# Layer 0's split activations moved to two areas with their own offsets in each stage, in a float32r decoder trunk

## The chip, the cores and the metric

The kernel runs on one core of a Trainium2 chip. The metric is the device time of one execution in microseconds. Before the change it is 2354.8 us, the median of three runs (2354.66 to 2355.55).

## What is computed

The reference is a decoder trunk of two layers over 272 tokens (16 meta tokens and 256 inputs) of width 2048, in float32. Layer 0 is a self-decoder with forgetting attention, layer 1 a cross-decoder with stick-breaking attention over a shared K/V; each is followed by a squared-ReLU MLP.

```python
D_MODEL = 2048; SEQ = 256; DEPTH = 2; N_HEADS = 16; D_FF = 4 * D_MODEL; N_META = 16

def squared_relu_mlp(h, w_up, w_down):
    u = h @ w_up
    return jnp.square(jax.nn.relu(u)) @ w_down

def reference(...):
    h = jnp.concatenate([meta, x], axis=1)
    for layer in range(DEPTH):
        a = rms_norm(h, norm_attn[layer])
        if layer < N_A_LAYERS:
            proj = a @ fox_w_in[i]
            q, k, v, f_logit = jnp.split(proj, [D_MODEL, 2 * D_MODEL, 3 * D_MODEL], axis=-1)
            ...
            o = forgetting_attention(split_heads(q), split_heads(k), split_heads(v), cum_logf)
            h = h + o.reshape(b, length, D_MODEL) @ fox_w_o[i]
        else:
            if layer == N_A_LAYERS:
                c = rms_norm(h, kv_norm)
                k_s, v_s = jnp.split(c @ w_kv, 2, axis=-1)
            ...
            q = split_heads(a @ sb_w_q[i])
            o = stick_breaking_attention(q, shared_k, shared_v)
            h = h + o.reshape(b, length, D_MODEL) @ sb_w_o[i]
        h = h + squared_relu_mlp(rms_norm(h, norm_mlp[layer]), w_up[layer], w_down[layer])
    return rms_norm(h, final_norm)[:, N_META:]
```

Nearly all of the arithmetic is in the products with the weight matrices.

## The kernel before

Activations lie feature-major in SBUF: the 128 partitions hold 128 features, a "chunk" c is one of 16 blocks of 128 features, and the tokens (272, or 256 where the meta tokens are no longer needed) run along the free dimension. `hT` is the residual stream.

To get float32 accuracy out of float32r products, each operand is split into a high part rounded to float32r and a low part with the rest, and a product W x is computed as three: whi·xhi + whi·xlo + wlo·xhi. An activation that feeds such products is a `Split` (L117): a tile of the pool `xs` (two buffers, tag "x") of 16 rows, one for each chunk, XROW = 576 floats (2304 bytes) apart. In each row hi starts at float XHI = 16 and lo follows directly after the n tokens of hi; `both` is the two together. `split_chunk` (L127) fills one chunk from hT: hi on ScalarE (L130), lo on VectorE (L131). `put_split` (L334) fills rows from attention outputs, and the evacuation of the MLP's up projection (L466) fills them from the squared ReLU.

The Splits by stage, in order: `a0` (input of layer 0's Q, K, V), `o0` (attention output, input of its projection), `m0` (input of the MLP's up projection), `u0_0` to `u0_3` (four quarters of the hidden layer, inputs of the down projection), then `a1` (256 tokens, queries of layer 1), `kv` (272 tokens, shared K and V), and layer 1's `o1`, `m1`, `u1_0` to `u1_3`, all of 256 tokens. a0, m0 and a1 lie in the first buffer of `xs`, o0, u0_0 to u0_3 and kv in the second.

`gemm_group` (L169) computes one group: 512 output features (four accumulators m of 128 features, in four PSUM banks) from all 2048 input features. It loads the weights in four blocks kb of 1 MB (`raw`, queue of SyncE), splits each half of a block into `whi` on ScalarE (L205) and `wlo` on VectorE (L206), and then runs over chunk kc and accumulator m. The variable `u` numbers the groups: 1 to 12 for Q, K, V of layer 0 (q, k, v for each of four groups of heads), 13 to 16 for its projection, 17 to 48 for its MLP (four quarters of four up and four down groups), 49 to 52 for layer 1's queries, 53 to 60 for K and V, the rest for layer 1. With 272 tokens (n = 272, a0 to u0_3 and kv) each (chunk, accumulator) takes three matmuls of 272 columns: L228 (whi, hi), L229 (whi, lo), L230 (wlo, hi); I call them a triple. There are 56 such groups of 64 triples, 3584 triples or 10752 matmuls. With 256 tokens (`pairs`) it takes two: L225 (whi, `both`, 512 columns) and L226 (wlo, hi, 256 columns). The framework's scheduler decides the final order on each engine within the data dependences, so L228 and L229 of several accumulators are sometimes grouped.

The forget gates (L281) multiply the same rows of a0 with weights of 16 columns, `wf_hi` and `wf_lo`, in three matmuls for each chunk (L286 to L288).

Addresses within a partition (bytes), as the framework allots them: the first buffer of `xs` starts at 91392, the second at 128256, both multiples of 256. So hi of every row starts 64 bytes past a multiple of 256; lo, 1088 bytes later where n is 272, starts at 128 past a multiple of 256. The weights `whi` and `wlo` start at multiples of 256 (66816, 79104 and on), and each 128x128 block of them is 512 bytes a partition; the gates' weights lie 64 bytes apart from chunk to chunk.

Of the kernel before, what the change touches and what calls it, by code (L numbers as in the profile page):

```python
# [9 lines left out]
F32 = mybir.dt.float32  # L10
F32R = mybir.dt.float32r
# [4 lines left out]
P = 128  # L16
D = 2048
NC = D // P
# [6 lines left out]
N_FF = 4  # L25
XROW = 576
XHI = 16

G_A0, G_M0, G_KV, G_A1, G_M1, G_FIN = range(6)

# [2 lines left out]
def yoco_kernel(ctx: ExitStack, tc: tile.TileContext, hT_in, gains, b_f, w_f, w_qkv0, w_o0, w_up, w_dn,  # L33
                w_kv, w_q1, w_o1, outT):
    nc = tc.nc
# [6 lines left out]
    xs = ctx.enter_context(tc.tile_pool(name="xs", bufs=2))  # L42
# [74 lines left out]
    class Split:  # L117


        def __init__(self, label, t0):  # L120
            n = T - t0
            self.t0 = t0
            rows = xs.tile([P, NC, XROW], F32R, tag="x", name=f"x_{label}")
            self.hi, self.lo = rows[:, :, XHI:XHI + n], rows[:, :, XHI + n:XHI + 2 * n]
            self.both = rows[:, :, XHI:XHI + 2 * n]

    def split_chunk(sp, gi, c):  # L127

# [40 lines left out]
    def gemm_group(wblk, sp, t0, evac, before={}, after={}, load_x=None, pairs=False, apart=()):  # L169

        uid[0] += 1
        u = uid[0]
        accs = [pacc.tile([P, 512], F32, tag="acc", name=f"acc_{u}_{m}") for m in range(4)]
        n = T - t0
        for kb in range(4):
            raw = wraw.tile([P, 4, 512], F32, tag="raw", name=f"raw_{u}_{kb}")  # L180
            src_w = wblk[kb].rearrange("p (k c) -> p k c", k=4)
            if kb in before:
                before[kb]()
            piece = 4 if load_x is None else (1, 2, 2, 4)[kb]
            for k0 in range(0, 4, piece):
                if load_x is not None:
                    load_x(range(4 * kb + k0, 4 * kb + k0 + piece))
                if load_x is not None and kb == k0 == 0:

                    for c0 in (0, 256):  # L190
                        nc.scalar.dma_start(raw[:, 0, c0:c0 + 256], src_w[:, 0, c0:c0 + 256])
                else:
                    nc.sync.dma_start(raw[:, k0:k0 + piece], src_w[:, k0:k0 + piece])
            piece = min(piece, 2)
            parts = []
            for hf in range(2):
                whi = wspl.tile([P, 2, 512], F32R, tag="whi", name=f"whi_{u}_{kb}_{hf}")
                wlo = wspl.tile([P, 2, 512], F32R, tag="wlo", name=f"wlo_{u}_{kb}_{hf}")
                boxes = [(o, piece, 0, 512) for o in range(0, 2, piece)]
                if load_x is not None and kb == hf == 0:  # L200
                    boxes[:1] = [(0, 1, 0, 256), (0, 1, 256, 512)]
                for o, no, c0, c1 in boxes:
                    src = raw[:, 2 * hf + o:2 * hf + o + no, c0:c1]
                    hp, lp = whi[:, o:o + no, c0:c1], wlo[:, o:o + no, c0:c1]
                    on_act = nc.scalar.activation(hp, src, AF.Copy)  # L205
                    on_dve = nc.vector.tensor_tensor(out=lp, in0=src, in1=hp.bitcast(F32), op=ALU.subtract)  # L206
                parts.append((whi, wlo))
            if kb in after:
                with tc.issue_after(on_act.ins), tc.issue_after(on_dve.ins):
                    after[kb]()  # L210
            order = [(kc, m) for hf in range(2) for m in range(4) for kc in range(2 * hf, 2 * hf + 2)]
            if load_x is not None and kb == 0:
                order = [(kc, m) for kc in range(4) for m in range(4)]
            if kb == 3:
                order = [(kc, m) for m in range(4) for kc in range(4)]
            for kc, m in order:
                whi, wlo = parts[kc // 2]
                k = 4 * kb + kc
                wh = whi[:, kc % 2, m * P:(m + 1) * P]
                wl = wlo[:, kc % 2, m * P:(m + 1) * P]  # L220
                first = kb == 0 and kc == 0
                last = kb == 3 and kc == 3
                hi, lo = sp.hi[:, k], sp.lo[:, k]
                if pairs and m not in apart:
                    nc.tensor.matmul(accs[m], wh, sp.both[:, k], start=first, stop=False)  # L225
                    nc.tensor.matmul(accs[m][:, :n], wl, hi, start=False, stop=last)  # L226
                else:
                    nc.tensor.matmul(accs[m][:, :n], wh, hi, start=first, stop=False)  # L228
                    nc.tensor.matmul(accs[m][:, :n], wh, lo, start=False, stop=False)  # L229
                    nc.tensor.matmul(accs[m][:, :n], wl, hi, start=False, stop=last)  # L230
                if last:
                    evac(m, [accs[m][:, :n]] + ([accs[m][:, n:]] if pairs and m not in apart else []))
# [18 lines left out]
    def load_x(chunks):  # L251
        c0, n = chunks[0], len(chunks)
        nc.sync.dma_start(hT[:, c0:c0 + n, :], hT_in[:, c0:c0 + n, :])
        if c0 == 0:
            nc.sync.dma_start(g_sb, gains)
        for c in chunks:
            split_chunk(xa, G_A0, c)
# [82 lines left out]
    for g in range(4):  # L340
# [11 lines left out]
        if g == 0:  # L352
            gemm_group(w_qkv0[0], xa, 0, evac_q, after={kb: (lambda kb=kb: first_norm(kb)) for kb in range(4)}, load_x=load_x)
            forget_gates(box["rstd"])
        else:
            gemm_group(w_qkv0[3 * g], xa, 0, evac_q)
# [4 lines left out]
        def decays(j):  # L361

            for i, (o, n) in enumerate(((0, 144), (144, T))):
                nc.vector.scalar_tensor_tensor(out=s[:, j, o:o + n], in0=fk[:, j, :n],
                                               scalar=fq_sb[:, i, 4 * g + j:4 * g + j + 1],
                                               in1=maskA[:, o:o + n], op0=ALU.subtract, op1=ALU.add)

        gemm_group(w_qkv0[3 * g + 1], xa, 0, lambda m, acc: evac_kv(m, acc, kT),
                   after={j: (lambda j=j: decays(j)) for j in range(4)})

# [255 lines left out]
    a, y, t, rs = (fin[:, i, :] for i in range(4))  # L626
# [9 lines left out]
    for i in range(2):  # L636
        pr = patt.tile([P, 512], F32, tag="patt", name=f"pr_fin_{i}")
        for b in range(2):
            nc.tensor.matmul(pr[:, b * P:(b + 1) * P], rs[:, b:b + 1].to_broadcast([P, P]), ident,
                             start=True, stop=True)  # L640
        prs.append(pr[:, :S])
    ob = xs.tile([P, NC, XROW], F32, tag="x", name="ob")
    pr_sb = tmp.tile([P, T], F32, tag="relu", name="pr_sb")[:, :S]
    nc.scalar.copy(pr_sb, prs[1])
    for c, n in [(12, 1), (13, 1), (14, 1), (15, 1), (0, 2), (2, 2), (4, 2), (6, 2)]:
# [62 lines left out]
```

## Time and profile before

| | |
|---|---|
| median of three runs | 2354.8 us |
| profiled execution | 2355.27 us |
| its span, first to last instruction | 2353.6 us |
| granted TensorE clock, mean | 0.998 |
| TensorE busy | 2339.7 us, 99% |
| VectorE busy | 1343.7 us, 57% |
| ScalarE busy | 1056.2 us, 45% |
| DMA | 411.9 MB, mean 175 GB/s |

By stage, from the trace's first and last start on each Split:

| stage | Split | from, us | to, us | matmuls |
|---|---|---|---|---|
| Q, K, V of layer 0, with attention | a0 | 5.3 | 336.3 | 2304 |
| its projection | o0 | 336.4 | 436.2 | 768 |
| MLP up, four quarters | m0 | 436.3 | 1105.7 | 3072 |
| MLP down, four quarters in between | u0_0 to u0_3 | 532.4 | 1201.3 | 4 x 768 |
| queries of layer 1 | a1 | 1201.4 | 1293.1 | 512 |
| K, V of layer 1, with attention | kv | 1293.2 | 1521.6 | 1536 |
| layer 1's projection and MLP | o1, m1, u1_0 to u1_3 | 1521.7 | 2339.8 | 512 + 2048 + 4 x 512 + 16 |

A matmul's reported length includes a drain that overlaps the next one; the distance from one start to the next is what it costs the engine.

### The profile page before, as it was taken

How to read it: one execution, taken by the hardware profiler on the slowest of the kernel's cores; microseconds unless marked ns; L12 is line 12 of the kernel's file. 1: busy time of each engine (PE TensorE's matmuls, PEld its weight loads, DVE VectorE, ACT ScalarE, POOL GpSimd, SP SyncE). 2: the span in 40 equal slices, each digit the busy share in tenths (PEclk: the TensorE clock that was granted, in tenths of full speed). 3: DMA queues.
4: the chain of work that ended last, by engine and by line, in shares of the span. 5: the costliest groups of instructions: out<-in, count | busy, mean ns of one | idle time of the engine just before them, and what ended most of it. 6: DMA issues, size and time to landing. Idle time of an engine off the chain costs nothing.

```text
span 2353.6 us, 39103 instructions
## 1 busy us (share of the span) xinstructions
PE 2339.7 (99%) x16496; PEld 2207.5 (94%) x16496; DVE 1343.7 (57%) x1920; ACT 1056.2 (45%) x1471; POOL 33.4 (1%) x58
## 2 busy tenths in 40 slices
PE   9999999999999999999999999999999999999998
PEld 9999999999999999999998999988888888888887
DVE  7565555655454455455566555566555655655665
ACT  5434344544343344344445444445544543543543
POOL 1000000000000000000000000000000000000000
PEclk9999999999999999999999999999999999999999
DMA  6444444544555454545545444445545555455453
GB/s 231 157 157 171 171 162 162 179 176 168 178 177 179 171 188 162 186 172 179 180 162 196 162 145 143 146 175 179 193 178 186 196 179 197 174 187 196 178 197 125
DMA packets 61040, 411.92 MB, mean 175 GB/s; under 512 B 7089, under 2 KB 10049, under 8 KB 12097
## 3 DMA queue, kind: packets, MB, share of 16 engines
q1 hardware_dynamic: 58976, 406.27, 48.6%
q10 hardware_dynamic: 1888, 3.16, 0.4%
q8 instruction: 129, 2.11, 0.4%
q14 instruction: 47, 0.38, 0.0%
HBM read 407.29 MB, written 2.11 MB: 174 GB/s over the span
## 4 chain that ended last, share of the span: by engine, by line
PE 99%; DVE 0%; ACT 0%; DMA 0%; issue 0%; DVEq 0%; SPq 0%; ACTq 0%
PE acc L225 25%; PE acc L228 19%; PE acc L229 19%; PE acc L230 19%; PE acc L226 13%; PE ps L376 0%; PE pza L555 0%; PE pv L315 0%; PE po L438 0%; PE po L594 0%; PE pzb L556 0%; PE po L595 0%; PE po L439 0%; DMA g_sb<-gains 0%; ACT whi L205 0%; PE po L596 0%
## 5 line engine op out<-in xcount | busy, mean ns | idle before, releaser
L206 DVE TENSOR_TENSOR wlo<-raw,whi 128x1024 fp32r<-128x1024 f32 (+1 forms) x771 | 932.9, 1220 | 751.8 <-ACT whi L205 748.6
L205 ACT ACTIVATE whi<-raw 128x1024 fp32r<-128x1024 f32 (+1 forms) x771 | 803.2, 1054 | 1064.5 <-PE acc L229 669.8
L225 PE MATMUL acc<-x_m,whi 128*128 128x512 f32 x1024 | 343.2, 394 | 0.5 <-DVE relu L243 0.5
L225 PE MATMUL acc<-x_u,whi 128*128 128x512 f32 x1008 | 338.0, 394 | 0.0
L228 PE MATMUL acc<-x_u,whi 128*128 128x272 f32 (+1 forms) x1040 | 297.7, 289 | 0.0
L229 PE MATMUL acc<-x_u,whi 128*128 128x272 f32 (+1 forms) x1040 | 294.8, 286 | 0.0
L228 PE MATMUL acc<-x_m,whi 128*128 128x272 f32 x1024 | 293.4, 289 | 0.0
L229 PE MATMUL acc<-x_m,whi 128*128 128x272 f32 x1024 | 290.4, 286 | 0.0
L230 PE MATMUL acc<-x_u,wlo 128*128 128x272 f32 (+1 forms) x1040 | 285.2, 284 | 0.0
L230 PE MATMUL acc<-x_m,wlo 128*128 128x272 f32 x1024 | 280.7, 284 | 0.0
L226 PE MATMUL acc<-x_m,wlo 128*128 128x256 f32 x1024 | 252.7, 282 | 0.0
L226 PE MATMUL acc<-x_u,wlo 128*128 128x256 f32 x1008 | 247.6, 281 | 0.0
L228 PE MATMUL acc<-x_a,whi 128*128 128x272 f32 x768 | 222.6, 294 | 0.8 <-ACT x_a L130 0.8
L229 PE MATMUL acc<-x_a,whi 128*128 128x272 f32 x768 | 220.2, 291 | 0.0
L225 PEld LDWEIGHTS acc<-x_m,whi 128*128 128x128 f32 x1024 | 185.0, 188 | 30.3 <-DVE relu L243 0.9
L230 PE MATMUL acc<-x_a,wlo 128*128 128x272 f32 x768 | 211.2, 288 | 0.0
L226 PEld LDWEIGHTS acc<-x_m,wlo 128*128 128x128 f32 x1024 | 192.3, 188 | 19.6 <-DVE wlo L206 4.7
L225 PEld LDWEIGHTS acc<-x_u,whi 128*128 128x128 f32 x1008 | 182.4, 188 | 29.8
L226 PEld LDWEIGHTS acc<-x_u,wlo 128*128 128x128 f32 x1008 | 189.3, 188 | 15.8 <-DVE wlo L206 1.5
L228 PEld LDWEIGHTS acc<-x_u,whi 128*128 128x128 f32 x1040 | 195.5, 188 | 0.2
L229 PEld LDWEIGHTS acc<-x_u,whi 128*128 128x128 f32 x1040 | 195.1, 188 | 0.1
L228 PEld LDWEIGHTS acc<-x_m,whi 128*128 128x128 f32 x1024 | 192.5, 188 | 0.0
(249 smaller groups left out, 3601.3 us busy)
## 6 DMA issues: line engine op xcount, KB each, us to landing
raw<-w_up SPq DMA_DIRECT2D x128, 1024.0 KB, 4.8
raw<-w_dn SPq DMA_DIRECT2D x128, 1024.0 KB, 4.8
raw<-w_qkv SPq DMA_DIRECT2D x45, 1024.0 KB, 4.8
raw<-w_o SPq DMA_DIRECT2D x32, 1024.0 KB, 4.8
raw<-w_kv SPq DMA_DIRECT2D x32, 1024.0 KB, 4.8
raw<-w_q SPq DMA_DIRECT2D x16, 1024.0 KB, 4.9
fk<-f_dram ACTq DMA_DIRECT2D x4, 544.0 KB, 5.7
raw<-w_qkv SPq DMA_DIRECT2D x4, 512.0 KB, 8.2
```

The costliest lines, as they stand in the source:

```text
L205: on_act = nc.scalar.activation(hp, src, AF.Copy)
L206: on_dve = nc.vector.tensor_tensor(out=lp, in0=src, in1=hp.bitcast(F32), op=ALU.subtract)
L225: nc.tensor.matmul(accs[m], wh, sp.both[:, k], start=first, stop=False)
L226: nc.tensor.matmul(accs[m][:, :n], wl, hi, start=False, stop=last)
L228: nc.tensor.matmul(accs[m][:, :n], wh, hi, start=first, stop=False)
L229: nc.tensor.matmul(accs[m][:, :n], wh, lo, start=False, stop=False)
L230: nc.tensor.matmul(accs[m][:, :n], wl, hi, start=False, stop=last)
```

## The change

Splits named in `FIRST_ROWS` (all with 272 tokens) get another layout: hi in one area of the tile and lo in a second area, in both with rows 288 floats (1152 bytes) apart. hi's area starts a floats into the tile, lo's area XLO + b = 4672 + b floats into it; each Split has its own pair (a, b), with a of 0 or 16 and b of 0, 16, 32 or 48, so that each of the eight pairs occurs once. The other Splits keep their rows, cut out of the now larger tile (9344 floats and not 9216). In `gemm_group`, groups of 272 tokens with an even number u multiply whi with lo first and then with hi; groups with an odd number keep the order hi, lo. The final output tile `ob`, of the same pool, is cut to the old shape.

```diff
+FIRST_ROWS = {"a0": (16, 32), "o0": (0, 16), "m0": (16, 48), "u0_0": (0, 32), "u0_1": (16, 0), "u0_2": (0, 48),
+              "u0_3": (16, 16), "kv": (0, 0)}
+XLO = 4672
+XSIZE = XLO + 64 + NC * 288
...
-            rows = xs.tile([P, NC, XROW], F32R, tag="x", name=f"x_{label}")
-            self.hi, self.lo = rows[:, :, XHI:XHI + n], rows[:, :, XHI + n:XHI + 2 * n]
-            self.both = rows[:, :, XHI:XHI + 2 * n]
+            rows = xs.tile([P, XSIZE], F32R, tag="x", name=f"x_{label}")
+            if label in FIRST_ROWS:
+
+                a, b = FIRST_ROWS[label]
+                self.hi, self.lo = (rows[:, o:o + NC * 288].rearrange("p (c t) -> p c t", c=NC)[:, :, :n]
+                                    for o in (a, XLO + b))
+            else:
+                rows = rows[:, :NC * XROW].rearrange("p (c t) -> p c t", c=NC)
+                self.hi, self.lo = rows[:, :, XHI:XHI + n], rows[:, :, XHI + n:XHI + 2 * n]
+                self.both = rows[:, :, XHI:XHI + 2 * n]
...
-                    nc.tensor.matmul(accs[m][:, :n], wh, hi, start=first, stop=False)
-                    nc.tensor.matmul(accs[m][:, :n], wh, lo, start=False, stop=False)
+                    a, b = (hi, lo) if u % 2 else (lo, hi)
+                    nc.tensor.matmul(accs[m][:, :n], wh, a, start=first, stop=False)
+                    nc.tensor.matmul(accs[m][:, :n], wh, b, start=False, stop=False)
                     nc.tensor.matmul(accs[m][:, :n], wl, hi, start=False, stop=last)
...
-    ob = xs.tile([P, NC, XROW], F32, tag="x", name="ob")
+    ob = xs.tile([P, XSIZE], F32, tag="x", name="ob")[:, :NC * XROW].rearrange("p (c t) -> p c t", c=NC)
```

The first buffer of `xs` stays at 91392, the second moves from 128256 to 128768.

## The prediction

> **What bounds the kernel now.** The profile's page comes first, its busy shares, the granted clock and the chain:
>
> ```profile
> span 2353.6 us, 39103 instructions
> PE 2339.7 (99%) x16496; PEld 2207.5 (94%) x16496; DVE 1343.7 (57%) x1920; ACT 1056.2 (45%) x1471; POOL 33.4 (1%) x58
> PEclk9999999999999999999999999999999999999999
> PE 99%; DVE 0%; ACT 0%; DMA 0%; issue 0%; DVEq 0%; SPq 0%; ACTq 0%
> ```
>
> TensorE is busy from end to end at full clock and is the whole chain; VectorE stands at 57%, the 16 DMA engines at about half. Nothing but the pace of the matmuls can move the time. Their groups, from the same page:
>
> ```profile
> L228 PE MATMUL acc<-x_m,whi 128*128 128x272 f32 x1024 | 293.4, 289 | 0.0
> L229 PE MATMUL acc<-x_m,whi 128*128 128x272 f32 x1024 | 290.4, 286 | 0.0
> L230 PE MATMUL acc<-x_m,wlo 128*128 128x272 f32 x1024 | 280.7, 284 | 0.0
> ```
>
> Three products of one shape differ by 3 and 2 ns, and none was idle before. The reported length holds a drain that overlaps the next matmul, so I go by the distance between starts, in the timeline of one steady stretch (columns: start, length, instruction):
>
> ```profile
> 427.36 0.29 PE L228 MATMUL acc<-x_o,whi 128*128 128x272 f32 x1
> 427.49 0.29 PE L229 MATMUL acc<-x_o,whi 128*128 128x272 f32 x1
> 427.61 0.28 PE L230 MATMUL acc<-x_o,wlo 128*128 128x272 f32 x1
> 427.74 0.29 PE L228 MATMUL acc<-x_o,whi 128*128 128x272 f32 x1
> ...
> 428.48 0.29 PE L228 MATMUL acc<-x_o,whi 128*128 128x272 f32 x1
> ```
>
> From 427.36 to 428.48 are three triples of products in 1.12 us: 373.3 ns a triple. The trace's starts to the nanosecond split it: 126.7 from L228's start to the next, 125.0 after L229, 121.7 after L230 (each is the length above less 162). It is nearly the same in all of layer 0, over addresses that differ by multiples of 256 bytes: the three repeat whatever the chunk and the weights are. So products of one shape, weights of one shape and no wait still differ by 5 ns, 4%.
>
> What differs is where the rows start. The hi rows start 64 bytes past a multiple of 128, the lo rows on one (from the tiles' addresses and XHI). Sorted by the row read before and the row read now, the intervals are: 64 after 64, 126.7; 64 after 0, 121.7; 0 after 64, 125.0. The fourth case, 0 after 0, occurs only near the start, where the scheduler put four L229 in a row:
>
> ```profile
> 10.06 0.67 PE L228 MATMUL acc<-x_a,whi 128*128 128x272 f32 x4
> 10.56 0.66 PE L229 MATMUL acc<-x_a,whi 128*128 128x272 f32 x4
> 11.06 0.67 PE L230 MATMUL acc<-x_a,wlo 128*128 128x272 f32 x4
> ...
> 12.08 0.66 PE L229 MATMUL acc<-x_a,whi 128*128 128x272 f32 x4
> 12.58 0.54 PE L230 MATMUL acc<-x_a,wlo 128*128 128x272 f32 x3
> ```
>
> Inside the two runs of L229 the trace has 126, 128, 122 and 127, 127, 123 ns: mean 125.5, six cases.
>
> **The change part by part.** No instruction is added, taken away or moved: built, both programs have the same instructions in the same order on each of the five engines, and the same number of waits. Three things differ.
>
> The order of the products in even groups: L228 and L229 read lo, then hi. Over a triple the same neighbours occur (hi after hi, lo after hi, hi after lo), so by the table this costs 0. It would cost if lo, which VectorE makes after ScalarE's hi, were late: the split on VectorE takes about 0.49 us. But each stage of layer 0 starts with an odd group, hi first, and an even group finds rows that are a whole group old (64 triples of 0.373 us, 24 us). Without that cover it would be about 0.5 us for each of the 28 even groups, 14 us; I take 0.
>
> The pool: each of two x buffers grows by 512 bytes, so the second moves by 512 and tmp and att by 1024. Offsets within 512 stay as they are; layer 1 keeps its rows and costs 0. ScalarE and VectorE write as many elements as before, to rows of unit step as now, and what a write may cost more is covered by their idle time (1297 us of the span on ACT, 1010 on DVE); without that cover 10 ns more on each of the 2 x 128 row writes of layer 0's eight tiles would be 2.6 us.
>
> The rows: this is the real part. hi starts at 4a bytes and lo at 18688 + 4b past the buffer's start, both buffers on a multiple of 256, so the places within 128 are (hi, lo): a0 (64, 0), o0 (0, 64), m0 (64, 64), u0_0 (0, 0), u0_1 (64, 0), u0_2 (0, 64), u0_3 (64, 64), kv (0, 0). With the table, a triple is:
> - (64, 0): 126.7 + 125.0 + 121.7 = 373.3, as now. a0 and u0_1, 768 + 256 triples: 0.
> - (64, 64): 3 x 126.7 = 380.0, 6.7 more. m0 and u0_3, 1024 + 256 triples: +8.5 us.
> - (0, 0): 3 x 125.5 = 376.5, 3.2 more. u0_0 and kv, 256 + 512 triples: +2.4 us.
> - (0, 64): 125.5 + 121.7 + 125.0 = 372.2, 1.2 less. o0 and u0_2, 512 triples: -0.6 us.
>
> Sum +10.3 us. The profiled execution took 2355.27 us (span 2353.6 and 1.7 around it), 0.5 above the median of 2354.8: 2355.3 + 10.3 = 2365.6, and on the median 2365.1. I take **2365**.
>
> What the trace does not show is the place within 256. Until now hi was always at 64 and lo at 128; rows 1152 bytes apart move every second chunk by 128. The nearest rows are the forget gates' products, which read the same hi and lo rows with weights of 16 columns whose address moves by 64 a chunk:
>
> ```profile
> 35.98 0.28 PE L286 MATMUL pf<-x_a,wf_hi 128*16 128x272 f32 x1
> ...
> 36.35 0.29 PE L286 MATMUL pf<-x_a,wf_hi 128*16 128x272 f32 x1
> ...
> 37.47 0.28 PE L286 MATMUL pf<-x_a,wf_hi 128*16 128x272 f32 x1
> ```
>
> From 35.98 to 37.47 are four triples; to the nanosecond 370, 375, 374 and 375, and the next four repeat it within 1. So the place against the weights does matter, and bounds a triple below by 370 (121.7 or less for every second matmul); above, the costliest steady neighbours are 380. Over 3584 triples: 3584 x -3.3 = -12 us, and 3584 x 6.7 = +24 us. Layer 1's pairs are farther off: single ones take 339 to 360 ns for 768 columns, but their mean, about 351, is 0.457 ns a column, as layer 0's 373.3 / 816. They widen nothing.
>
> The Trainium skill speaks against any effect: SBUF — State Buffer, "Who interferes with whom", gives TensorE one read port for the moving operand and an independent one for weight loads, and says that TensorE waits for nobody; by it the sum would be 0. The gate triples differ with the weights' address, so the trace does not agree to the last 1%.
>
> **The rivals.** First, the place within 128 is only a label for "the same place as the row before", and a shift by 128 counts as another place. Then a neighbour at the same place within 256 costs 126.7 and any other 123.3, the mean of 125.0 and 121.7. Counted over the built program, same places are 3597 of 10752 now (a third) and 3484 after, because in m0 two thirds of the neighbours lie 128 apart: 113 x 3.3 ns, -0.4 us, time 2355. For it: the two runs of 0 after 0 start close to 127. Against it: 0 after 0 falls to 122 and 123 at the end of a run, so place itself counts. The skill's rule ends at the same 2355.
>
> Second, faster: the pace follows the moving row's place against the weights' place, and the new rows fall on good ones. Place: every triple of layer 0, most of all m0's 1024. Price: 370 in place of 373.3 everywhere, -12 us, **2343**. For it: the gates' first triple. Against: three of four gate triples are no better than now, and m0 has lost the alternation that makes its L229 and L230 cheap. It decides over the table once the mean triple falls below 373.3, that is, once it gives back 2.9 ns of the table's mean 376.2.
>
> Third, much slower: lo and hi of one chunk now lie some 18.7 KB apart and not 1088 bytes; if it is their nearness that makes L229 and L230 cheap, each interval is 126.7, +24 us, 2379. For it: the cheapest interval follows the step from lo back to hi. Against: L228 follows a hi row 2304 bytes away and L230 to L230 runs at the same row give 126.7 too, so distance plays no part in them.
>
> **How the numbers follow.** The table 0.50 (2365), no net effect 0.17 (2355), faster 0.25 (2343), all at 126.7 0.08 (2379). A difference of 0.2%, 4.7 us, can be told from none. Faster 0.25, the same 0.17, slower 0.50 + 0.08 = 0.58. The table's own range is 2359 to 2372: the six cases of 0 after 0 may be off by 3 ns either way in the 768 triples of (0, 0), 7 us; behind both runs of L229 the next 64 after 0 took 125 and not 121.7, which in the 512 triples of (0, 64) would be 1.7 us, within that. Over all cases 2343 to 2380.
>
> **What would show it.** The lines of the groups in m0 (acc from x_m at 272 columns) should all have a mean of 289 ns, in place of 289, 286 and 284; u0_3's starts should lie 126.7 apart, u0_1's triples and a0's stay at 373. In the table's case kv's and u0_0's intervals average 125.5. If even and odd chunks of one stage differ, the place within 256 counts and the table is wrong; if even and odd groups differ, the order counts. The forecast fails if m0's triples, 6.8 of the 10.3 us, are not longer than 373.

## The result, and the profile after

The changed kernel takes 2366.4 us (median of three runs, 2366.0 to 2367.1), where before took 2354.8: a ratio of 1.0048, 95% interval 1.0031 to 1.0065, 11.6 us slower. The forecast was 2365, slower.

The page of the changed kernel, the lines that answer to those shown of before (its line numbers have moved: L241, L242, L243 are the three products, L237 and L238 those of layer 1's pairs):

```profile
span 2364.6 us, 39103 instructions
PE 2350.9 (99%) x16496; PEld 2219.1 (94%) x16496; DVE 1344.0 (57%) x1920; ACT 1056.0 (45%) x1471; POOL 33.2 (1%) x58
PEclk9999999999999999999999999999999999999999
PE 99%; DVE 0%; ACT 0%; DMA 0%; issue 0%; DVEq 0%
L241 PE MATMUL acc<-x_m,whi 128*128 128x272 f32 x1024 | 293.1, 288 | 0.0
L242 PE MATMUL acc<-x_m,whi 128*128 128x272 f32 x1024 | 292.1, 288 | 0.0
L243 PE MATMUL acc<-x_m,wlo 128*128 128x272 f32 x1024 | 285.1, 289 | 0.0
```

The clock, the instructions and the other engines' work are the same; TensorE is busy for 11.2 us more and the span is 11.0 us longer. m0's groups are now at 288, 288 and 289 ns, where they were at 289, 286 and 284. So the matmuls themselves have another pace, and nothing waits.

How much in which stage is seen in windows laid inside the stages (columns: stretch and its length, TensorE's busy time and number of matmuls, clock, DMA). Before, in the order a0, m0, u0_1, u0_3, kv:

```profile
40.00:330.00 290.00, 290.00 (x2280) 1.00 0.46 161
640.00:720.00 80.00, 80.00 (x645) 1.00 0.52 179
735.00:815.00 80.00, 80.00 (x646) 1.00 0.50 176
1120.00:1200.00 80.00, 80.00 (x645) 1.00 0.50 178
1310.00:1520.00 210.00, 210.00 (x1607) 1.00 0.42 146
```

and after:

```profile
40.00:330.00 290.00, 290.00 (x2266) 1.00 0.46 161
640.00:720.00 80.00, 80.00 (x638) 1.00 0.51 179
735.00:815.00 80.00, 80.00 (x643) 1.00 0.51 176
1120.00:1200.00 80.00, 80.00 (x641) 1.00 0.51 178
1310.00:1520.00 210.00, 210.00 (x1599) 1.00 0.42 147
```

Fewer matmuls fit into every window, in a0 as well, which the forecast had left as it was. From the starts of the matmuls (mean distance from a start to the next, leaving out those over 140 ns, which stand behind a wait or beside another kind of matmul) and the stages' lengths:

| stage | ns a matmul before | after | forecast, us | measured, us |
|---|---|---|---|---|
| a0 | 124.65 | 125.61 | 0 | +2.5 |
| o0 | 124.50 | 125.37 | -0.3 | +0.7 |
| m0 | 124.45 | 125.90 | +6.8 | +4.5 |
| u0_0 | 124.45 | 125.50 | +0.8 | +0.8 |
| u0_1 | 124.44 | 124.94 | 0 | +0.4 |
| u0_2 | 124.44 | 125.21 | -0.3 | +0.6 |
| u0_3 | 124.45 | 125.26 | +1.7 | +0.6 |
| kv | 124.66 | 125.91 | +1.6 | +1.8 |

The sum came out, +11.8 (added before rounding) against +10.3, but not from the terms that were to make it: the stages of the places (64, 64) lost less, u0_0 as much as forecast, all others more. Outside of these stages the span became 0.8 us shorter, so that it grew by 11.0. And the steady rhythm is gone. In m0 an odd group runs like this (start, length, instruction):

```profile
460.20 0.29 PE L243 MATMUL acc<-x_m,wlo 128*128 128x272 f32 x1
460.34 0.28 PE L241 MATMUL acc<-x_m,whi 128*128 128x272 f32 x1
460.46 0.29 PE L242 MATMUL acc<-x_m,whi 128*128 128x272 f32 x1
460.59 0.28 PE L243 MATMUL acc<-x_m,wlo 128*128 128x272 f32 x1
```

From start to start it alternates between 121 and 133 ns (0.14 at 460.20, 0.12 at 460.34, 0.13 at 460.46; the view rounds to 10 ns). Every row here stands at 64 within 128, so the forecast's table has a single value for it, 126.7. The mean of 121 and 133 is close to it, 126.65, but the even groups of the same stage average 125.15. The place within 128 alone is not what decides. The same product, L243, takes 133 ns in one triple (at 460.20) and 121 in the next (at 460.59), which by the kernel's loop is the next chunk: even and odd chunks differ, which the forecast had named as the sign that the place within 256 counts. Its sign for the order, that even and odd groups differ, is there as well.

### The profile page after: what moved, and what is told of

It reads as the page before. It is cut to its first block, busy times and chain, and to the rows that moved or that the text cites. A ratio compares the mean times of both kernels' runs of the same rounds, so it can differ in the third digit from the quotient of the medians.

```text
span 2364.6 us, 39103 instructions
## 1 busy us (share of the span) xinstructions
PE 2350.9 (99%) x16496; PEld 2219.1 (94%) x16496; DVE 1344.0 (57%) x1920; ACT 1056.0 (45%) x1471; POOL 33.2 (1%) x58
## 4 chain that ended last, share of the span: by engine, by line
PE 99%; DVE 0%; ACT 0%; DMA 0%; issue 0%; DVEq 0%
PE acc L237 25%; PE acc L241 19%; PE acc L243 19%; PE acc L242 19%; PE acc L238 13%; PE ps L389 0%; PE pza L568 0%; PE pv L328 0%; PE po L451 0%; PE po L607 0%; PE po L608 0%; PE pzb L569 0%; ACT whi L217 0%; PE po L452 0%; DMA raw<-w_qkv 0%; PE po L609 0%
## 5 line engine op out<-in xcount | busy, mean ns | idle before, releaser
L237 PE MATMUL acc<-x_m,whi 128*128 128x512 f32 x1024 | 343.0, 394 | 0.5 <-DVE relu L256 0.5
L237 PE MATMUL acc<-x_u,whi 128*128 128x512 f32 x1008 | 338.0, 394 | 0.0
L241 PE MATMUL acc<-x_u,whi 128*128 128x272 f32 (+1 forms) x1040 | 297.1, 288 | 0.0
L242 PE MATMUL acc<-x_u,whi 128*128 128x272 f32 (+1 forms) x1040 | 296.5, 287 | 0.0
L241 PE MATMUL acc<-x_m,whi 128*128 128x272 f32 x1024 | 293.1, 288 | 0.0
L242 PE MATMUL acc<-x_m,whi 128*128 128x272 f32 x1024 | 292.1, 288 | 0.0
L243 PE MATMUL acc<-x_u,wlo 128*128 128x272 f32 (+1 forms) x1040 | 288.2, 287 | 0.0
L243 PE MATMUL acc<-x_m,wlo 128*128 128x272 f32 x1024 | 285.1, 289 | 0.0
L238 PE MATMUL acc<-x_m,wlo 128*128 128x256 f32 x1024 | 252.6, 282 | 0.0
L238 PE MATMUL acc<-x_u,wlo 128*128 128x256 f32 x1008 | 247.6, 281 | 0.0
L241 PE MATMUL acc<-x_a,whi 128*128 128x272 f32 x768 | 222.9, 295 | 0.6 <-ACT x_a L142 0.6
L242 PE MATMUL acc<-x_a,whi 128*128 128x272 f32 x768 | 221.9, 293 | 0.0
L237 PEld LDWEIGHTS acc<-x_m,whi 128*128 128x128 f32 x1024 | 185.0, 188 | 30.2 <-DVE relu L256 0.9
L243 PE MATMUL acc<-x_a,wlo 128*128 128x272 f32 x768 | 213.2, 291 | 0.0
L238 PEld LDWEIGHTS acc<-x_m,wlo 128*128 128x128 f32 x1024 | 192.3, 188 | 19.6 <-DVE wlo L218 4.7
L237 PEld LDWEIGHTS acc<-x_u,whi 128*128 128x128 f32 x1008 | 182.5, 188 | 29.8
L238 PEld LDWEIGHTS acc<-x_u,wlo 128*128 128x128 f32 x1008 | 189.3, 188 | 15.8 <-DVE wlo L218 1.5
L241 PEld LDWEIGHTS acc<-x_u,whi 128*128 128x128 f32 x1040 | 195.7, 188 | 0.2
L242 PEld LDWEIGHTS acc<-x_u,whi 128*128 128x128 f32 x1040 | 195.7, 188 | 0.1
L242 PEld LDWEIGHTS acc<-x_m,whi 128*128 128x128 f32 x1024 | 193.7, 189 | 0.0
```

Source lines behind the costliest of these rows:

```text
L241: nc.tensor.matmul(accs[m][:, :n], wh, a, start=first, stop=False)
L242: nc.tensor.matmul(accs[m][:, :n], wh, b, start=False, stop=False)
```

## The experiments

Theory A is the forecast's table: an interval is set by the place within 128 bytes of the row read and of the row read before; the order costs nothing. Theory B: it is places within 256 that count, and rows that shift by 128 from chunk to chunk break the old rhythm. After the first four runs B was made sharper: by theory C the interval hangs on where the moving row stands against the weights that are loaded at the same time; theory D says that it is the moving rows alone.

**The order undone.** The changed kernel, hi before lo in all groups.

```diff
-                    a, b = (hi, lo) if u % 2 else (lo, hi)
+                    a, b = hi, lo
```

> The changed kernel with the order hi, lo in every group. Theory A (the table: the place of a row within 128 bytes after the place of the row before sets each interval, the order costs nothing): as the changed kernel, 2366 us within 1. Theory B (the rows' places within 256 bytes, which now alternate from chunk to chunk, break a rhythm that was the same in every triple, and order and places together choose another one): each stage runs at the mean that its odd groups have in the changed kernel (a0 125.9, o0 125.2, m0 126.65, u0 125.0, 124.5, 124.8, 125.3, kv 125.9 ns a matmul), which sums to some 14 us over before, 2368 to 2369 us.

Measured: 2366.35 us, ratio to before 1.0047 (1.0032 to 1.0062), so as the changed kernel. A's total holds, B's of 2368 to 2369 is 2 us too high. B's means come out within 0.2 ns in a0 (125.75), o0 (125.3), the four u0 (125.0, 124.35, 124.8, 125.25) and kv (125.9), but not in m0. There whole groups run at 125.6 and others, of the same code and places, at 126.65: first four groups 125.6, then eight at 126.65, then four at 125.6. One layout can have two rhythms. The groups at 125.6 come behind o0 and u0_2, both at (0, 64) within 128, those at 126.65 behind u0_0 and u0_1, both with lo at 0; whether the stage before picks the rhythm was not tested. With the new rows the order does move single stages: u0_0 runs at 125.5 with two orders and at 125.0 with one, m0 at 125.9 and 126.1. It is the sum over the stages that stays the same.

**The orders alone**, on the kernel before.

```diff
-                    nc.tensor.matmul(accs[m][:, :n], wh, hi, start=first, stop=False)
-                    nc.tensor.matmul(accs[m][:, :n], wh, lo, start=False, stop=False)
+                    a, b = (hi, lo) if u % 2 else (lo, hi)
+                    nc.tensor.matmul(accs[m][:, :n], wh, a, start=first, stop=False)
+                    nc.tensor.matmul(accs[m][:, :n], wh, b, start=False, stop=False)
```

> The kernel before with the two orders alone, rows as they were. Theory A: 0, 2355 us, 124.45 ns a matmul in even groups as in odd ones. Theory B says nothing of it by itself; if the order has a price of its own without the new rows, even groups (half of 10752 matmuls) move by some tenths of a ns, 1 ns would be 5.4 us.

Measured: 2355.35 us against 2355.33 for before, ratio 1.0 (0.9991 to 1.001); 124.45 ns in even and odd groups of the MLP alike. With the rows of before, the order costs nothing.

**The rows alone.** Two areas, rows 1152 bytes apart, one pair for all stages, so that hi is at 64 and lo at 0 within 128 as before; within 256 they are at (64, 128) in even chunks, as before, and at (192, 0) in odd ones.

```diff
-FIRST_ROWS = {"a0": (16, 32), "o0": (0, 16), "m0": (16, 48), "u0_0": (0, 32), "u0_1": (16, 0), "u0_2": (0, 48),
-              "u0_3": (16, 16), "kv": (0, 0)}
+FIRST_ROWS = {k: (16, 32) for k in ("a0", "o0", "m0", "u0_0", "u0_1", "u0_2", "u0_3", "kv")}
...
-                    a, b = (hi, lo) if u % 2 else (lo, hi)
+                    a, b = hi, lo
```

> Two areas and rows 1152 bytes apart, but every stage with a0's pair (places 64 and 0 within 128, as before) and the order hi, lo. Theory A: as before, 2355 us, triples of 373.3 ns. Theory B: every stage as a0's odd groups in the changed kernel, 125.9 ns a matmul, 1.5 over before times 10752, +16 us, 2371 us.

Measured: 2373.71 us, ratio 1.0077 (1.0060 to 1.0094), 18.4 us over before. A falls: it has 0 here. B has the direction, but 125.9 ns and 2371 us were too low. The groups of m0 in this kernel (L240 to L242 are the three products):

```profile
L240 PE MATMUL acc<-x_m,whi 128*128 128x272 f32 x1024 | 295.0, 290 | 0.0
L241 PE MATMUL acc<-x_m,whi 128*128 128x272 f32 x1024 | 293.1, 288 | 0.0
L242 PE MATMUL acc<-x_m,wlo 128*128 128x272 f32 x1024 | 284.2, 288 | 0.0
```

The lengths were 289, 286, 284, at the same places within 128. The interval is 126.67 ns in all of the MLP; kv, with the same pair in the same buffer as u0, but with attention's matmuls in between, has 124.7 to 126.0 by group. So the rows alone cost 18 us, and the change's other pairs, run in the same order hi, lo, cost 7.4 less (2373.71 to 2366.35).

**The old rows with other offsets**, a pair for each stage, so that places within 256 stay fixed.

```diff
+ROWS = {"a0": (16, 304), "o0": (32, 304), "m0": (0, 272), "u0_0": (0, 272), "u0_1": (0, 288), "u0_2": (0, 304), "u0_3": (16, 304), "kv": (32, 304)}
...
-            self.hi, self.lo = rows[:, :, XHI:XHI + n], rows[:, :, XHI + n:XHI + 2 * n]
+            a, b = ROWS.get(label, (XHI, XHI + n))
+            self.hi, self.lo = rows[:, :, a:a + n], rows[:, :, b:b + n]
```

> The old rows, 2304 bytes apart, so that places within 256 are the same in every chunk, with another pair in each stage, order hi, lo. Places of hi and lo within 256: a0 and u0_3 (64, 192), o0 and kv (128, 192), m0 and u0_0 (0, 64), u0_1 (0, 128), u0_2 (0, 192). Theory A: triples of 380 in a0 and u0_3, 372.2 in o0, m0, u0_0, u0_2 and kv, 376.5 in u0_1; in all +5 us, 2360 us. Theory B: each stage has one rhythm of its own that repeats in every triple, with two or three values of interval in it and hardly any spread; which mean it has isn't said, but pairs with the same places within 128 (m0 and u0_2; o0 and kv against m0) may differ.

Measured, in one execution: 2362.4 us. ns a matmul: (64, 192) 124.55 in u0_3 and 124.7 in a0; (128, 192) 125.7 in o0 and kv; (0, 64) 125.75 in m0 and u0_0; (0, 128) 124.45 in u0_1; (0, 192) 125.0 in u0_2. Neither theory's picture is whole: A's 126.7 for (64, 64) within 128 is 124.6 here, and the three pairs that A holds for equal are 125.0 to 125.75. B's claim that places within 256 matter holds, and one pair gives the same mean in both buffers. But B's spread is wrong: in m0 the values run from 119 to 130.

**The weights moved and not the rows.** The tile `pad` behind the constants goes behind the weights' pool, which then starts 128 bytes lower; in a second kernel it grows to 48 floats, with another 48 behind the weights, so that the weights go 64 bytes up and x 256. Rows of x stay where they were within 256.

```diff
-    align = ctx.enter_context(tc.tile_pool(name="align", bufs=1))
     wspl = ctx.enter_context(tc.tile_pool(name="wspl", bufs=3))
+    align = ctx.enter_context(tc.tile_pool(name="align", bufs=1))
```

> The kernel before with the split weights 128 bytes lower (at 128 past a multiple of 256), x where it was. Theory C (the interval hangs on the moving row's place against the place of the weights that are loaded at the same time, within 256): another repeating rhythm than 126.7, 125.0, 121.7, that of x at (192, 0) with the weights at 0, whose mean no run has shown; 0.3 ns or more off 124.45 would be 3 us or more. Theory D (the moving rows' own places, alone and after each other, weights without effect): 124.45 ns and the same three values, 2355 us.

```diff
     wspl = ctx.enter_context(tc.tile_pool(name="wspl", bufs=3))
+    align2 = ctx.enter_context(tc.tile_pool(name="align2", bufs=1))
...
-    pad = align.tile([P, 32], F32, name="pad")
+    pad = align.tile([P, 48], F32, name="pad")
     nc.gpsimd.memset(pad, 0.0)
+    pad2 = align2.tile([P, 48], F32, name="pad2")
+    nc.gpsimd.memset(pad2, 0.0)
```

> The kernel before with the split weights 64 bytes higher, x at the same places within 256. Theory C: against the weights x now stands as the pair (0, 64) did in m0 and u0_0 of the kernel with the old rows and other offsets, so 125.75 ns a matmul with that run's values (124, 125, 129, 130, 126, 127), 1.3 x 10752 = 14 us, about 2369 us. Theory D: 124.45 ns, 2355 us.

Measured, in one execution each: 2358.0 us with 128, 2369.3 with 64, beside 2355.6 for before. In a long window over the MLP (m0 and the u0 together), first before, then the weights 128 lower, then 64 higher:

```profile
540.00:1100.00 560.00, 560.00 (x4503) 1.00 0.50 177
```

```profile
540.00:1100.00 560.00, 560.00 (x4501) 1.00 0.50 177
```

```profile
540.00:1100.00 560.00, 560.00 (x4455) 1.00 0.49 175
```

With 64, every stage of layer 0 has 125.74 to 125.77 ns, within 0.05 of what (0, 64) gave when the rows were moved. D falls: no row moved within 256, and 14 us came. That x went 256 bytes up is no rival, since its rows lie 9 x 256 bytes apart and before has its three values in every chunk. Nor is it the splitting of the weights on ScalarE and VectorE at the same time: the intervals of m0 in which both were idle for at least half the time average 125.6 ns here, 126.6 with the rows alone and 124.5 before.

With 128, where x has not moved at all, the mean is as before in layer 0 (124.4 to 124.6), but the three steady values are gone (they run from 119 to 130), another rhythm as C says and against D, and layer 1's products of 512 columns rose from 231.9 to 233.05 ns; the 2.4 us of the total are there (909.8 to 912.2 us). A window of layer 1's MLP has this many matmuls (before, 2955):

```profile
1720.00:2240.00 520.00, 520.00 (x2948) 1.00 0.51 187
```

**The weights alternate too.** First the rows as in "the rows alone" (64 and 128, then 192 and 0 in odd chunks), and the weights of odd chunks 128 bytes on; then the weights alone, with the rows of before. (Two small tiles of layer 1, `sc` and `ec`, have one buffer here and not two, to make room.)

```diff
-                whi = wspl.tile([P, 2, 512], F32R, tag="whi", name=f"whi_{u}_{kb}_{hf}")
-                wlo = wspl.tile([P, 2, 512], F32R, tag="wlo", name=f"wlo_{u}_{kb}_{hf}")
+                whi = wspl.tile([P, 2, 544], F32R, tag="whi", name=f"whi_{u}_{kb}_{hf}")[:, :, :512]
+                wlo = wspl.tile([P, 2, 544], F32R, tag="wlo", name=f"wlo_{u}_{kb}_{hf}")[:, :, :512]
```

and, in the first of the two (x's pool starts 64 bytes later, so that a row start of 0 stands where 64 stood):

```diff
-XHI = 16
+XHI = 0
+XLO = 4624
...
+            if label in FIRST:
+                self.hi = rows[:, :NC * 288].rearrange("p (c t) -> p c t", c=NC)[:, :, :n]
+                self.lo = rows[:, XLO - 16:XLO - 16 + NC * 288].rearrange("p (c t) -> p c t", c=NC)[:, :, 16:16 + n]
```

> Rows 1152 bytes apart with the one pair (places 64 and 128 in even chunks, 192 and 0 in odd ones) and order hi, lo, as in the kernel with the rows alone (2373.7 us), but the weights of odd chunks also 128 bytes on, so that within a chunk x stands against its weights as before. Theory C: at least two of three intervals of a triple see the old relation, so clearly below that kernel's 126.67 ns, and 124.45 if the chunk's change counts for nothing. Theory D: 126.67 ns as there, 2374 us.

> The kernel before, rows of x as they were, but the weights of odd chunks 128 bytes on. Theory C: x against the weights changes from chunk to chunk just as with the new rows, so near 126.7 ns a matmul in the MLP, 2372 to 2374 us. Theory D: 124.45 ns, 2355 us.

Measured, in one execution each: 2357.2 us with both, 2360.5 with the weights alone. The window over the MLP, first of the rows alone, then of both, then of the weights alone:

```profile
540.00:1100.00 560.00, 560.00 (x4423) 1.00 0.49 173
```

```profile
540.00:1100.00 560.00, 560.00 (x4487) 1.00 0.50 177
```

```profile
540.00:1100.00 560.00, 560.00 (x4470) 1.00 0.50 177
```

The same rows that ran at 126.67 ns run at 124.86 once their weights move along: 1.8 of the 2.2 ns are given back, as C says. The weights alone cost 0.9 ns (125.35) where C was read as 2.2: the direction is right, the size is not. While the last matmul of a chunk runs, the next chunk's weights load, so the two ways of alternating differ at that point; whether this explains the difference wasn't tried apart.

Both totals are lower than layer 0 alone would make them: layer 1's stages of 256 tokens took 906.0 and 906.1 us, before 909.8.

**Finer places, and layer 1.** Old rows, a pair for each stage as above, and another row start in layer 1's stages. (`a` and `b` are read from `ROWS` as in the kernel with other offsets.)

```diff
+ROWS = {"a0": (16, 296), "o0": (8, 288), "m0": (0, 288), "u0_0": (24, 296), "u0_1": (8, 280), "u0_2": (20, 292), "u0_3": (12, 284), "kv": (24, 304),
+        "a1": (0, 256), "o1": (32, 288), "m1": (48, 304), "u1_0": (0, 256), "u1_1": (32, 288), "u1_2": (8, 264), "u1_3": (24, 280)}
...
-            self.both = rows[:, :, XHI:XHI + 2 * n]
+            self.both = rows[:, :, a:a + 2 * n]
```

> The old rows and order, with shifts of 16 and 32 bytes tried in layer 0 and other places of the rows of 256 tokens in layer 1, a pair for each stage. Places of (hi, lo) in bytes within 256: a0 (64, 160), o0 (32, 128), m0 (0, 128), u0_0 (96, 160), u0_1 (32, 96), u0_2 (80, 144), u0_3 (48, 112), kv (96, 192); layer 1's row start: a1 and u1_0 0, o1 and u1_1 128, m1 192, u1_2 32, u1_3 96, where it was 64. Theory C (place against the weights): m0 repeats the 124.45 that the pair (0, 128) had in u0_1 of the kernel with other offsets; the others are open, between 123.3 (the best of the forget gates' chunks) and 126.7. In layer 1, row start 192 must be like the weights moved by 128 (233.0 and 118.4 ns for the 512- and 256-column products, 231.7 and 118.4 before) and start 0 like the weights moved by 64 (233.1 and 117.2). Theory D (no part for the weights): 231.7 and 118.4 at any start. A place that is 1 ns cheaper in all of layer 0 would save 11 us.

Measured, in one execution: 2364.6 us. The check on C holds: (0, 128) gives 124.42 in m0; in layer 1 a row start of 192 gives 232.9 and 118.4, one of 0 gives 232.9 to 233.5 and 117.3 to 117.4, as the moved weights did. No place of layer 0 beat 124.42: (48, 112) 124.55, (96, 160) 124.65, (80, 144) 124.8, (32, 96) 125.35, (96, 192) 125.7, (64, 160) 126.2, (32, 128) 126.4. The gain of 11 us that was open isn't there. In layer 1 a row start of 128 gave 232.3 to 232.6 and 119.7 to 120.0, one of 96 gave 233.2 and 118.45, both more than before. One of 32 gave 231.25 and 117.7 in its one stage, less than that stage's 232.1 and 118.4 before; it wasn't run in all of them.

**The version that beats both.** The kernel before, with the weights of odd chunks 128 bytes on in the groups of 256 tokens alone (and, as in the two kernels with alternating weights, one buffer for `sc` and `ec`).

```diff
-                whi = wspl.tile([P, 2, 512], F32R, tag="whi", name=f"whi_{u}_{kb}_{hf}")
-                wlo = wspl.tile([P, 2, 512], F32R, tag="wlo", name=f"wlo_{u}_{kb}_{hf}")
+                step = 544 if pairs else 512
+                whi, wlo = (wspl.tile([P, 1088], F32R, tag=t, name=f"{t}_{u}_{kb}_{hf}")
+                            [:, :2 * step].rearrange("p (k c) -> p k c", k=2)[:, :, :512] for t in ("whi", "wlo"))
```

> The kernel before, with the weights of odd chunks 128 bytes on in the groups of 256 tokens alone. Theory C: layer 0 as before (124.45 ns), layer 1 as in the kernel with alternating weights, whose stages of 256 tokens took 906.1 us where before took 909.8: 3.7 us less, 2351.6 us, 0.16%. Theory D: 2355 us.

Measured: 2351.9 us against 2355.3 for before beside it, ratio 0.9985 (0.9976 to 0.9994). A window of layer 1's MLP, before and then this kernel:

```profile
1720.00:2240.00 520.00, 520.00 (x2955) 1.00 0.52 188
```

```profile
1720.00:2240.00 520.00, 520.00 (x2967) 1.00 0.52 189
```

Twelve more matmuls in 520 us, 0.4%, with the MLP of layer 0 at 124.45 ns as before. In layer 1 the products of 512 columns went from 231.9 to 231.5 ns and those of 256 from 118.4 to 117.4, so the gain is in the pace. It is small, but the interval lies clear of 1.

## Why the prediction was right or wrong

The time was right, and so were three of its steps: TensorE's pace is all that moves (its busy time takes up the 11 us, and the instructions stand as they did); the two orders cost 0 (2355.35 against 2355.33 with the rows of before; with the new rows 0 in the sum, by stages that cancel); the pool's shift and layer 1 cost 0 (layer 1's stages of 256 tokens took 909.5 us, before 909.8).

The step that failed is the table, "sorted by the row read before and the row read now", as a rule of places within 128. Its three measured values were right for before, but before had only one relation within 256 to show them in. The rows alone, at the same places within 128, cost 18.4 us where the table had 0, and the old rows at (64, 192) cost 0.1 ns where it had 2.2. Two of the forecast's own signs say the same: a0's triples were to stay at 373 and took 376.8, u0_3's were to take 380 and took 375.8. The sum came near because the eight pairs together ran at 125.6 ns, 1.1 over the 124.5 of before, and 1.1 ns times 10752 is 11.8 us; the table had 10.3 us, spread over other stages. That nearness was luck: in a0 it missed 2.5 us, in m0 2.3 the other way, and over all layouts tried the stages ran at means from 124.35 to 126.67 ns.

The unknown that was named, the place within 256, was the one that counted, and the forget gates' triples were the row that told of it: 369 to 376 in the last eight of them, with the weights' address alone moving within 256 (370 to 380 in the others). The forecast used them for the range's lower end and the price of a rival, and not in its sum. Moving the weights by 64 shows directly that their place can cost 14 us. Whether it counts while the weights are loaded, as C words it, was not told apart from their place as such.

Of the rivals, no effect fell in both its forms. That a neighbour 128 away counts as another place is refuted by the rows alone: there fewer neighbours share a place within 256 than before, which by this rival makes it faster, and it was the slowest kernel. The Trainium skill's rule (SBUF — State Buffer, "Who interferes with whom") of an independent read port for weight loads does not describe the last 1% here: with the weights 64 bytes on, every stage of layer 0 was 1.3 ns a matmul slower. The faster rival, good places against the weights, had the right mechanism and the wrong sign for these places: no layout tried in layer 0 averaged under 124.3 ns over a stage. The rival at 126.7 in every interval is what the rows alone come close to, by another cause: when the weights moved along, with lo as far from hi as there, 124.86 came back.

## What to carry to other kernels

Where matmuls run without a wait and still differ by a few ns, compare starts, sort them by the address of the moving row and by that of the weights, and move one of them at a time: 64 bytes were worth 14 us here. A rule read from one layout holds for the places that this layout shows; a price for another layout should be taken from the rows in which the second address moves, however few. In layer 0 no layout was clearly better than that of before, in which every chunk stands alike against its weights (124.35 ns was the best stage of any). In layer 1 alternating weights saved 3.7 us, so this is no rule for other shapes: run both.

## What the runs showed of the hardware that was not expected

The place of the split weights within 256 bytes changes the pace of matmuls that read the same rows: 124.45 ns at 0, 125.76 at 64, 124.4 to 124.6 at 128 (272 columns). Moving the rows the other way gives the same mean: (0, 64) with the weights at 0 gave 125.75.

One layout can hold two rhythms for whole stages: with one order, m0's groups ran at 125.6 or at 126.65 ns with nothing else changed, and with the rows alone kv ran at 124.7 to 126.0 where the MLP ran at 126.67. What picks the rhythm, and by what mechanism the two places together set the pace, stays open.
